# Other pads in on-chip memory before the activation tiles of a two-block model

## The chip, the cores and the metric

The kernel runs on one core of one Trainium2 chip. The metric is the device time of one execution in microseconds (us). Before the change the median of three runs is 1627.86 us (1627.2 to 1629.0). The activations are float32; the large matrix products are made with the fp32r form of TensorE, in which one product of two float32 operands is put together from three products of rounded parts.

## The reference, cut to what matters

Two blocks follow each other on 256 tokens of width 1024. The first has two layers; the second, one.

```
for l in range(2):
    x = x + 0.5 * swiglu(rms_norm(x), w_gate_up, w_down)      # 1024 -> 2*2816 -> 1024   (ffn1)
    u = rms_norm(x) @ w_in
    y = concat(ssd_mixer(u), mlstm_mixer(u), rwkv7_mixer(u))  # 2048 wide
    x = x + y @ w_out
    x = x + 0.5 * swiglu(rms_norm(x), w_gate_up, w_down)      # (ffn2)
x = rms_norm(x)
# second block, one layer, modulated by a vector c
h = rmsnorm(x) * (1 + sc1) + sh1
q, k, v, u, c_gate, b_gate = split(h @ w_in_2)
mixed = concat(rmsnorm(attention(q, k, v)), rmsnorm(b_gate * conv(c_gate * u)))
x = x + gt1 * (mixed @ w_out_2)
h = rmsnorm(x) * (1 + sc2) + sh2
val, gte = split(conv(h @ w_up_2))
x = x + gt2 * ((silu(gte) * val) @ w_down_2)
out = rmsnorm(x)
```

All weights are read once from HBM, as float32.

## The kernel before, in words

Activations lie transposed, features on the 128 partitions and the 256 tokens along the free dimension. The weights come in blocks of 128 x 128. Seven blocks form a chunk: `fetch` loads it into `raw` (SyncE's queue), `chunk` splits it with ScalarE into the rounded part `whi` (L134) and with VectorE into the rest `wlo` (L135). Four buffers of `whi` and four of `wlo` go round. `mm` makes three matmuls of one block and one activation tile (L153, L154, L155): high by high, high by low, low by high; each loads 128 columns of weights and streams 256 columns of activations. "Product" below means one such matmul. There are some 11,400 of them, and the program has 12,670 matmuls in all.

The activations of a product are split in the same way, and the high and the low part lie behind each other in one tile:

- `pair()` makes the input tiles of the dense products, under two names in turn. `pair1` holds the unnormalised input of the first four output tiles of a stage (`xg`: the products can start before the norm's statistics are there, and are scaled behind), `pair0` the normalised input (`xn`). For the second block's attention the normalised input lies in `pair1`.
- `hp` holds the hidden activations of a feed-forward stage (22 tiles of 128 features), the input of its down stage. Each of the five feed-forward stages has its own pool and its own `hp`.
- `m0`, `m1` hold the input of the second block's `w_out`; the first block's `w_out` inputs are tiles of the mixers' ring `w2` (`w` in the profile).
- `xgh`, `xgl` hold the second block's unnormalised inputs with two columns more (258).

Memory is given out from pools that are stacked: `const`, `weights`, `act`, then one pool for the stage (`ffn`, `mix`, `attn`), and from the second layer's ffn2 on a pool `later` below it, which holds the attention bias `ab` and `xgh`, `xgl`. `gap(pool, n)` takes n bytes of each partition from a pool and has GpSimd clear them (L261); nothing reads them. Its only effect is where the tiles behind it lie. The table `GAPS` sets n for each place.

The code's order sets the order of the work on each engine; there is no planner. Weights are taken from the front of the stream, so the down stage of a feed-forward follows its gate and up products without a break.

Of the kernel before, what the change touches and what calls it, by code (L numbers as in the profile page):

```python
# [37 lines left out]
GD_AHEAD = 1  # L38
BOOST = (1, 1, 1, 1, 1)
DENSE = 0.34  # L40
GAPS = {"xg": 448, "xn": 192, "mix": 288, "ffn": (384, 128, 448, 192, 448), "attn": 256}
W_OUT = ((("rwkv0", "rwkv1"), (12, 13, 14, 15)), (("ssd",), (0, 1, 2, 3, 4, 5, 6, 7)), (("mlstm",), (8, 9, 10, 11)))

IN_PAIRS = "k0 r0 v0 r2 k2 v2 xb8 xb0 dtg xb2 xb4 xb6 z0 z2 z4 xm0 z6 xm2 o0 o2".split()
# [33 lines left out]
def _program(tc, a, order, dbg=None):  # L78
# [5 lines left out]
    def pool(name, bufs=1, **kw):  # L84
        return es.enter_context(tc.tile_pool(name=name, bufs=bufs, **kw))
# [172 lines left out]
    def gap(pool, n):  # L258
        if n:
            turn.append(0)  # L260
            G.memset(pool.tile([128, n // 4], F32, name=f"gap{len(turn)}"), 0.0)  # L261
# [3 lines left out]
    def pair(dtype=F32R):  # L265
        pairs.append(0)
        return act.tile([128, 2, DT, T], dtype, name=f"pair{len(pairs) % 2}")
# [4 lines left out]
    def new_acc():  # L272
        return act.tile([128, 2, T], F32, name="acc", bufs=2)
# [47 lines left out]
    def ffn(l, which, acc, xg, next_gain):  # L321
        with tc.tile_pool(name=f"ffn{which}{l}", bufs=1) as fp:
            gu, dn = f"ffn{which}_w_gate_up", f"ffn{which}_w_down"
            gap(fp, GAPS["ffn"][2 * l + which - 1])
            hp = fp.tile([128, 2, FT, T], F32R, name="hp")
# [59 lines left out]
    def mixers(l, acc, xg):  # L385
# [10 lines left out]

        gap(mp, GAPS["mix"])
        nka = mp.tile([128, 4], F32, name="nka")
# [740 lines left out]
    def modulate(rb, gain, shift):  # L1139
        xn = pair()  # L1140
        for j in range(DT):
            n = tmp()[:, 0]
            V.scalar_tensor_tensor(n, x[:, j], gain[:, j:j + 1], rb, op0=OP.mult, op1=OP.mult)
            S.activation(xn[:, 0, j], n, AF.Identity, bias=shift[:, j:j + 1])
            V.scalar_tensor_tensor(xn[:, 1, j], n, shift[:, j:j + 1], xn[:, 0, j].bitcast(F32),
                                   op0=OP.add, op1=OP.subtract)
        return xn
# [12 lines left out]
    def second(accs, xg):  # L1160
        rb, rb2 = stat_rstd(accs, D, EPS, chain=True)
        with tc.tile_pool(name="attn", bufs=1) as mp:
            xn = modulate(rb2, a1[:, 0], mod[:, 0:8])
            gap(mp, GAPS["attn"])
            mixed = [mp.tile([128, 2, 4, T], F32R, name=f"m{i}") for i in range(2)]
# [102 lines left out]
        with tc.tile_pool(name="ffn_2", bufs=1) as fp:  # L1268
            rb, = stat_rstd([acc], D, EPS)
            xn = modulate(rb, a1[:, 1], mod[:, 24:32])  # L1270
            gap(fp, GAPS["ffn"][4])
            hp = fp.tile([128, 2, FT, T], F32R, name="hp")
# [40 lines left out]
    acc = new_acc()  # L1313
    gap(act, GAPS["xg"])
    xg = pair()
    gap(act, GAPS["xn"])
    for j in range(0, DT, 2):
# [8 lines left out]
    later = None  # L1326
    for l in range(LAYERS):
        acc, xg = ffn(l, 1, acc, xg, f"mix_norm{l}")
        dbg(f"xa{l}", x)
        acc, xg = mixers(l, acc, xg)  # L1330
        dbg(f"xb{l}", x)
        if l == LAYERS - 1:
            later = pool("later")
            ab = later.tile([128, 8, 384], F32, name="ab")
        acc, xg = ffn(l, 2, acc, xg, f"ffn1_norm{l + 1}" if l + 1 < LAYERS else None)
        dbg(f"xc{l}", x)
# [161 lines left out]
```

## Time and profile before

| | |
|---|---|
| median of three runs | 1627.86 us |
| profiled execution | 1627.1 us, span 1625.3 us |
| TensorE busy with matmuls | 1584.9 us, 13,660 instructions |
| VectorE, ScalarE, GpSimd busy | 1161.4, 1000.1, 47.5 us |
| mean granted TensorE clock | 0.989 of full speed |
| HBM read | 287.51 MB, 178 GB/s over the span |

The profiled execution takes 1.8 us more than the span from its first to its last instruction. The share of busy time of TensorE counts pipelined matmuls, so it tells that a matmul was under way, not how densely they follow each other. How densely is read from the starts: in a stretch where products follow each other without a wait, the time from the first to the last start over the number of products in between is the pace, in ns for one product. In a row of the view by tile, the starts are those of every third product (the lines L153, L154 and L155 take turns), so n instructions of one line span 3(n - 1) steps.

### The profile page before, as it was taken

The numbers are of one execution on the slowest core, as the hardware profiler recorded it, in microseconds if no ns is written. First come the engines' busy times: TensorE is split into PE (matmuls) and PEld (weight loads), VectorE is DVE, ScalarE is ACT, GpSimd is POOL, SyncE is SP. The second block draws the span as 40 slices with busy tenths as digits, with TensorE's granted clock in tenths as the row PEclk, the third lists the DMA queues.
The fourth block names the chain that finished last, engine by engine and source line by source line (L and its number), as shares of the span: only waits on it lengthen the run. The fifth ranks groups of instructions, "written<-read, shape, count | busy, mean of one in ns | idle before, by whom it ended". The sixth has DMA issues, their size and how long they took to land.

```text
span 1625.3 us, 33775 instructions
## 1 busy us (share of the span) xinstructions
PE 1584.9 (98%) x13660; PEld 1516.4 (93%) x13660; DVE 1161.4 (71%) x1965; ACT 1000.1 (62%) x1692; POOL 47.5 (3%) x68
## 2 busy tenths in 40 slices
PE   8999999999999999999999899999999999999998
PEld 7999988878999999999998887799999998999997
DVE  7865679856787755787568975688785676798853
ACT  6554576887655454545458788765554566587753
POOL 0000001000000000000000100000000000000000
PEclk9999989999999999999999999999999999999999
DMA  7866633333357766597563333436886653556662
GB/s 252 306 195 190 204 118 123 101 112 116 115 181 244 242 187 194 185 329 260 183 194 125 115 106 117 127 117 216 288 306 185 185 166 113 159 162 190 187 189 72
DMA packets 106717, 290.81 MB, mean 179 GB/s; under 512 B 15640, under 2 KB 28096, under 8 KB 106432
## 3 DMA queue, kind: packets, MB, share of 16 engines
q1 hardware_dynamic: 106272, 288.12, 55.9%
q8 instruction: 107, 1.75, 0.4%
q10 hardware_dynamic: 288, 0.52, 0.1%
q14 instruction: 50, 0.41, 0.1%
HBM read 287.51 MB, written 1.09 MB: 178 GB/s over the span
## 4 chain that ended last, share of the span: by engine, by line
PE 77%; issue 13%; DVE 5%; ACT 2%; DMA 1%; POOL 1%; SPq 0%; DVEq 0%; POOLq 0%; ACTq 0%
PE d L155 21%; PE d L153 21%; PE d L154 21%; DVE wlo L135 1%; DMA ada<-ada 1%; PE m L691 1%; PE m L754 1%; PE m L1064 1%; POOL stm L212 1%; PE m L1068 1%; PE m L736 1%; PE st L221 1%; PE m L705 1%; ACT whi L134 1%; PE m L1066 1%
## 5 line engine op out<-in xcount | busy, mean ns | idle before, releaser
L135 DVE TENSOR_TENSOR wlo<-raw,whi 128x896 fp32r<-128x896 f32 x544 | 590.4, 1089 | 245.1 <-ACT whi L134 242.3
L153 PE MATMUL d<-pair,whi 128*128 128x256 f32 x2672 | 753.2, 282 | 4.8 <-ACT whi L134 2.1
L155 PE MATMUL d<-pair,wlo 128*128 128x256 f32 x2672 | 753.8, 282 | 1.8 <-DVE wlo L135 1.8
L154 PE MATMUL d<-pair,whi 128*128 128x256 f32 x2672 | 752.9, 282 | 0.1
L134 ACT CAST whi<-raw 128x896 fp32r<-128x896 f32 x544 | 511.5, 943 | 348.3 <-PE d L154 254.0
L153 PEld LDWEIGHTS d<-pair,whi 128*128 128x128 f32 x2672 | 508.8, 190 | 14.8 <-issue 5.9
L155 PEld LDWEIGHTS d<-pair,wlo 128*128 128x128 f32 x2672 | 508.1, 190 | 7.2 <-DVE wlo L135 2.9
L154 PEld LDWEIGHTS d<-pair,whi 128*128 128x128 f32 x2672 | 508.5, 190 | 3.0 <-issue 1.4
L154 PE MATMUL d<-hp,whi 128*128 128x256 f32 x880 | 246.6, 280 | 0.0
L155 PE MATMUL d<-hp,wlo 128*128 128x256 f32 x880 | 246.1, 280 | 0.0
L153 PE MATMUL d<-hp,whi 128*128 128x256 f32 x880 | 246.1, 280 | 0.0
L155 PEld LDWEIGHTS d<-hp,wlo 128*128 128x128 f32 x880 | 166.2, 189 | 0.0
L154 PEld LDWEIGHTS d<-hp,whi 128*128 128x128 f32 x880 | 166.1, 189 | 0.0
L153 PEld LDWEIGHTS d<-hp,whi 128*128 128x128 f32 x880 | 166.1, 189 | 0.0
L205 ACT CAST hp<-h 128x256 fp32r<-128x256 f32 x88 | 35.4, 406 | 90.9 <-DVE h L345 90.8
L1124 DVE SCALAR_TENSOR_TENSOR adasum<-ada,sc,adasum 128x1024 f32<-128x1024 f32 x42 | 53.8, 1281 | 14.4 <-DMA ada<-ada 14.4
L206 DVE TENSOR_TENSOR hp<-h,hp 128x256 fp32r<-128x256 f32 x88 | 36.7, 421 | 15.3 <-ACT hp L205 14.5
L1157 DVE SCALAR_TENSOR_TENSOR up<-raw,par,up 128x255 f32<-128x255 f32 (+1 forms) x88 | 37.2, 480 | 10.6 <-ACT raw L1153 10.3
L344 ACT ACTIVATE s<-d 128x256 f32<-128x256 f32 x80 | 30.2, 378 | 23.3 <-PE d L155 22.2
L345 DVE TENSOR_TENSOR h<-s,d 128x256 f32<-128x256 f32 x88 | 36.0, 415 | 3.8 <-ACT s L344 3.8
L155 PE MATMUL d<-w,wlo 128*128 128x256 f32 x128 | 37.1, 290 | 0.0
L154 PE MATMUL d<-w,whi 128*128 128x256 f32 x128 | 37.1, 290 | 0.0
(403 smaller groups left out, 1829.0 us busy)
## 6 DMA issues: line engine op xcount, KB each, us to landing
raw<-ws SPq DMA_DIRECT2D x544, 448.0 KB, 3.7
ada<-ada SPq DMA_DIRECT2D x48, 512.0 KB, 5.9
w<-da SPq DMA_DIRECT2D x16, 256.0 KB, 5.1
w<-small SPq DMA_DIRECT2D x10, 256.0 KB, 3.9
ab<-abias SPq DMA_DIRECT2D x1, 1536.0 KB, 7.1
x<-xT SPq DMA_DIRECT2D x4, 256.0 KB, 4.9
w<-da SPq DMA_DIRECT2D x8, 128.0 KB, 3.6
w<-dw SPq DMA_DIRECT2D x4, 256.0 KB, 5.5
```

The source lines that it names most:

```text
L134: S.copy(hi, raw)
L135: V.tensor_sub(lo, raw, hi.bitcast(F32))
L153: PE.matmul(p, h, xh, start=start, stop=False, skip_group_check=True)
L154: PE.matmul(p, h, xl, start=False, stop=False, skip_group_check=True)
L155: PE.matmul(p, lo, xh, start=False, stop=stop, skip_group_check=True)
L205: S.copy(hi, src)
L206: V.tensor_sub(lo, src, hi.bitcast(F32))
L212: G.tensor_tensor(dst, m, mhalf.to_broadcast([128, n]), op=OP.pow)
L344: S.activation(s, p[:, 0], AF.Silu)
L345: V.tensor_mul(h, s, p[:, 1])
L1124: V.scalar_tensor_tensor(acc, w, sc[:, k:k + 1], acc, op0=OP.mult, op1=OP.add)
L1157: V.scalar_tensor_tensor(dst[:, i, d:], raw[:, i, :T - d], P(w, 3 * j + k), dst[:, i, d:], op0=OP.mult, op1=OP.add)
```

## The change

The pads are set anew, and the pool `later` gets one. Nothing else is changed.

```diff
-GAPS = {"xg": 448, "xn": 192, "mix": 288, "ffn": (384, 128, 448, 192, 448), "attn": 256}
+GAPS = {"xg": 192, "xn": 192, "mix": 32, "ffn": (128, 128, 128, 0, 0), "attn": 0, "later": 256}
...
         if l == LAYERS - 1:
             later = pool("later")
+            gap(later, GAPS["later"])
             ab = later.tile([128, 8, 384], F32, name="ab")
```

The five numbers of `"ffn"` belong to layer 0's ffn1 and ffn2, layer 1's ffn1 and ffn2, and the second block's feed-forward. From them follow the start addresses, in bytes in each partition, as the built programs place the tiles. All eight weight buffers stay where they are; each of their blocks is 512 bytes long and begins at remainder 160 when divided by 256. The steps inside the activation tiles (1024 bytes from one feature tile to the next) keep the remainder of the first.

| tile (products) | before, remainder by 256 (by 512) | after, remainder by 256 (by 512) |
|---|---|---|
| `pair1` (1,056) | 93536: 96 (352) | 93280: 96 (96) |
| `pair0` (6,960) | 112224: 96 (96) | 111968: 96 (352) |
| `hp`, layer 0, ffn1 (528) | 129120: 96 (96) | 128608: 96 (96) |
| `hp`, layer 0, ffn2 (528) | 128864: 96 (352) | 128608: 96 (96) |
| `hp`, layer 1, ffn1 (528) | 129184: **160** (160) | 128608: **96** (96) |
| `hp`, layer 1, ffn2 (528) | 157728: **32** (32) | 157536: **96** (352) |
| `hp`, second block (528) | 157984: **32** (288) | 157536: **96** (352) |
| `w2`, eight in each layer (384) | 96 (96) | 96 (96) |
| `m0`, `m1` (192) | 157792, 165984: 96 (96) | 157536, 165728: 96 (352) |
| `xgh`, `xgl` (192) | 141024, 149280 | the same |

On TensorE, VectorE, ScalarE and SyncE the instructions stand in the same order as before. On GpSimd there are eight clearings of pads where there were ten. The next piece is GpSimd's order from the end of layer 1's mixers to the end of the program, before (-) and after (+), with the semaphores that an instruction waits for; `gap` is a pad, `stm` the statistics of a norm.

```order
-L261 MEMSET gap_13771 128x48 [waits DMAHW3_49,DMAHW1_49,DMAHW5_49,DMAHW0_49,DMAHW6_49,DVE_49,DMAHW7_49,PE_49,Pool_49]
-L212 TENSOR_TENSOR stm<-stm,mhalf 128x2 [waits DVE_49]
-L261 MEMSET gap_16201 128x64 [waits DMAHW2_49,DMAHW3_49,DMAHW1_49,DMAHW4_49,DMAHW0_49,DMAHW5_49,DVE_49,DMAHW7_49,PE_49,Pool_49]
+L261 MEMSET gap_13767 128x64 [waits DMAHW3_49,DMAHW1_49,DMAHW5_49,DMAHW0_49,DMAHW6_49,DVE_49,DMAHW7_49,PE_49,Pool_49]
+L212 TENSOR_TENSOR stm<-stm,mhalf 128x2 [waits DVE_49] x3
+L212 TENSOR_TENSOR stm<-stm,mhalf 128x2 [waits DVE_49,Pool_49] x2
 L212 TENSOR_TENSOR stm<-stm,mhalf 128x2 [waits DVE_49] x2
-L212 TENSOR_TENSOR stm<-stm,mhalf 128x2 [waits DVE_49,Pool_49] x2
-L261 MEMSET gap_17620 128x112 [waits DVE_49,PE_49]
-L212 TENSOR_TENSOR stm<-stm,mhalf 128x2 [waits DVE_49] x2
```

Of the three pads that stood here one is left, that of the pool `later`; the seven root calculations on the statistics are all still there, in the same order.

## Rows read from the trace of the kernel before

**Rows 1.** The page: span, TensorE's busy time, the chain that ended last.

```profile
span 1625.3 us, 33775 instructions
...
PE 1584.9 (98%) x13660; PEld 1516.4 (93%) x13660; DVE 1161.4 (71%) x1965; ACT 1000.1 (62%) x1692; POOL 47.5 (3%) x68
...
PE 77%; issue 13%; DVE 5%; ACT 2%; DMA 1%; POOL 1%; SPq 0%; DVEq 0%; POOLq 0%; ACTq 0%
```

**Rows 2.** Busy time by stretch; three down stages, then the last gate and up stage.

```profile
core 0: us, PE busy (x) PEld busy (x) DVE busy (x) ACT busy (x) POOL busy (x), PEclk, DMA share, GB/s
...
136.40:196.00 59.60, 59.60 (x528) 59.60 (x527) 34.83 (x42) 29.13 (x39) 0.00 (x0) 1.00 0.63 194
783.10:845.40 62.30, 62.30 (x521) 62.30 (x520) 34.55 (x42) 28.42 (x37) 0.00 (x0) 1.00 0.59 183
1243.20:1305.50 62.30, 62.30 (x528) 62.30 (x527) 36.76 (x47) 31.44 (x45) 0.00 (x0) 1.00 0.61 184
1455.00:1550.80 95.80, 95.80 (x815) 95.80 (x815) 83.47 (x152) 73.75 (x131) 0.00 (x0) 1.00 0.60 185
```

**Rows 3.** Tile hp, TensorE: count, ns min/median/max, first and last start (us).

```profile
L153 PE MATMUL d<-hp,whi x176: 276/276/276, 136.3 to 195.8; 128*128 128x256 f32 x176
...
L153 PE MATMUL d<-hp,whi x176: 276/276/276, 598.6 to 658.1; 128*128 128x256 f32 x176
...
L153 PE MATMUL d<-hp,whi x176: 280/283/283, 782.3 to 845.3; 128*128 128x256 f32 x176
...
L153 PE MATMUL d<-hp,whi x176: 279/281/285, 1243.1 to 1305.4; 128*128 128x256 f32 x176
...
L153 PE MATMUL d<-hp,whi x47: 279/281/285, 1551.0 to 1567.4; 128*128 128x256 f32 x47
...
L154 PE MATMUL d<-hp,whi x48: 279/281/362, 1569.1 to 1585.9; 128*128 128x256 f32 x48
```

**Rows 4.** Tiles pair, w and m, TensorE, uninterrupted stretches; the columns of rows 3.

```profile
L154 PE MATMUL d<-pair,whi x274: 276/276/282, 31.0 to 123.8; 128*128 128x256 f32 x137
...
L154 PE MATMUL d<-pair,whi x31: 276/276/282, 480.4 to 490.6; 128*128 128x256 f32 x31
...
L154 PE MATMUL d<-pair,whi x15: 276/276/369, 1238.0 to 1242.8; 128*128 128x256 f32 x15
...
L154 PE MATMUL d<-pair,whi x31: 281/281/281, 1125.4 to 1136.0; 128*128 128x256 f32 x31
...
L153 PE MATMUL d<-pair,whi x32: 281/281/281, 1320.6 to 1331.5; 128*128 128x256 f32 x32
...
L153 PE MATMUL d<-pair,whi x272: 281/281/384, 1454.8 to 1550.6; 128*128 128x256 f32 x136
...
L153 PE MATMUL d<-w,whi x32: 281/281/281, 462.6 to 473.5; 128*128 128x256 f32 x32
```

**Rows 5.** Groups by line, 136.3 to 196.3 us: count, busy us, mean ns, idle before.

```profile
L135 DVE TENSOR_TENSOR wlo<-raw,whi 128x896 fp32r<-128x896 f32 x26 | 28.4, 1092 | 23.2 <-ACT whi L134 23.1
L134 ACT CAST whi<-raw 128x896 fp32r<-128x896 f32 x26 | 24.6, 945 | 29.8 <-PE d L154 25.7 <-issue 3.5 <-ACT pair L302 0.3
```

**Rows 6.** Line L345, layer 0's and layer 1's ffn1; the columns of rows 3.

```profile
L345 DVE TENSOR_TENSOR h<-s,d x21: 411/414/422, 31.1 to 133.0; 128x256 f32<-128x256 f32 x21
...
L345 DVE TENSOR_TENSOR h<-s,d x21: 409/414/422, 675.0 to 777.9; 128x256 f32<-128x256 f32 x21
```

**Rows 7.** Groups by line on GpSimd, whole span; the columns of rows 5.

```profile
L212 POOL TENSOR_TENSOR stm<-stm,mhalf 128x2 f32<-128x2 f32 (+1 forms) x14 | 13.4, 957 | 356.5 <-DVE stm L238 347.2 <-DVE xgl L206 4.9 <-DVE stm L230 3.7
...
L261 POOL MEMSET gap<- 128x112 f32 (+5 forms) x10 | 1.5, 162 | 803.2 <-PE d L155 782.6 <-PE m L155 20.3 <-POOLq L1489 0.3
```

## The prediction

> **What bounds the kernel.** I read the page's head and chain first, then the busy time by stretch, then single tiles on TensorE. The page says that TensorE is busy 98% of the span and that 77% of the chain that ended last is its matmuls [rows 1]. Such a share doesn't tell how densely the matmuls follow each other. In the three down stages of rows 2 TensorE is busy without a hole (59.60 of 59.60 us, 62.30 of 62.30 us twice) at a granted clock of 1.00, its higher level of 2.4 GHz, while VectorE and ScalarE are busy 35 to 37 and 28 to 31 us, and the DMA engines 0.59 to 0.63 [rows 2]. So nothing is waited for there, and the time of such a stage is its number of products times their pace. Yet the same 528 products of the same shape take different times.
>
> The pace of each down stage comes from rows 3: 176 instructions of one line are 175 steps of three products, 525 products.
>
> - layer 0, ffn1 (`hp` at remainder 96): (195.8 - 136.3) / 525 = 113.3 ns
> - layer 0, ffn2 (remainder 96): (658.1 - 598.6) / 525 = 113.3 ns
> - layer 1, ffn1 (remainder 160, that of the weights): (845.3 - 782.3) / 525 = 120.0 ns
> - layer 1, ffn2 (remainder 32): (1305.4 - 1243.1) / 525 = 118.7 ns
> - second block (remainder 32): (1567.4 - 1551.0) / 138 = 118.8 ns, and behind the next break (1585.9 - 1569.1) / 141 = 119.1 ns
>
> Remainders here are by 256. By 512 the two fast tiles lie at 96 and at 352 and have one pace, so 256 is the period that the rows support.
>
> Placement isn't all of it. Tiles that lie at 96 throughout have two paces [rows 4]: `pair` at 31.0 to 123.8 makes 92.8 / 819 = 113.3 ns, at 1454.8 to 1550.6 95.8 / 813 = 117.8 ns, and the mixers' `w` at 462.6 (10.9 / 93) 117 ns with 0.1 us of rounding. The median duration of one shows which it is, 276 or 281 ns. The pace is taken at a stretch's beginning and mostly kept until a wait breaks it. Of the eight stretches of `pair` with over 400 products in a row, the first and last of which are the first and sixth row of rows 4, seven have the fast pace. In short ones it is less even: the products behind the norm's statistics at ffn2's start (`pair1`, then `pair0`) run fast in layer 0 (480.4 to 490.6, 10.2 / 90) and slow at the corresponding place of layer 1 (1125.4 to 1136.0, 10.6 / 90) [rows 4]. I call them fast (113.3) and slow (117.8).
>
> **The change, part by part.** By 256, three tiles move in relation to the weights: the `hp` of layer 1's ffn1 (160 to 96), of its ffn2 and of the second block (32 to 96). All other inputs of products keep their remainder by 256; several move by 256.
>
> 1. Layer 1's ffn1 down. Its products follow without a break from `pair`, which has the fast pace in all long stretches of both layers but the second block's, and at 96 both down stages that follow fast products keep it [rows 3]. 63.0 us become 59.5: -3.5 us. At the slow pace it would be 528 x (120.0 - 117.8) = -1.2 us.
> 2. Layer 1's ffn2 down. The products before it run at 276 ns, the fast pace (1238.0 to 1242.8) [rows 4]. 62.3 us become 59.5: -2.8 us; at the slow pace -0.5 us.
> 3. The second block's down. The products before it run slow [rows 4], so the first 142, up to the first break by transposes, take the slow pace: 142 x 0.9 ns = -0.1 us. The other 386 begin anew behind each of four breaks. All fast would be 386 x 5.4 = -2.1 us, all slow -0.3 us. Seven long stretches in eight speak for one end, the pair at 480.4 and 1125.4 for a coin; I take two thirds fast, -1.5 us. Together -1.6 us.
> 4. The tiles that move by 256 or more with the remainder kept: 0. `pair1` at 352 by 512 runs at both paces (slow at 1320.6), `pair0` at 96 by 512 too (slow at 1454.8, fast at 31.0) [rows 4], so neither place excludes one. The bounds are in the rivals.
> 5. VectorE and ScalarE tiles in the feed-forward pools move in relation to 256 as well. L345 takes 414 ns in the median in layer 0's and in layer 1's ffn1, whose pools stood 64 apart [rows 6]: 0. The second block's pool alone has the conv of the up stage; a change of its speed would meet a VectorE that is busy 83.5 of 95.8 us beside a full TensorE [rows 2], so it stays covered up to some 12 us.
> 6. Two clearings fewer on GpSimd: all ten take 1.5 us [rows 7], each at a stage's turn, on an engine that then idles until VectorE has the statistics ready; its 14 root calculations waited 347 of 356 us for VectorE [rows 7]. Value 0, at most 0.3 us (two of 162 ns) either way. The new clearing in `later` stands where one of the removed stood, with the same engines in its wait; only the root calculations are queued behind it.
>
> What becomes late next: a faster down stage wants a chunk every 21 x 113.3 = 2.38 us. Splitting one takes 945 ns on ScalarE and 1092 ns on VectorE, on two engines and with four buffers, and layer 0's ffn1 down did so for 26 chunks [rows 5] with TensorE never idle [rows 2]. So the cover holds.
>
> Sum: 3.5 + 2.8 + 1.6 = 7.9 us off the profiled execution's own 1627.1 us: 1619.2 us. The median of the runs stands 0.8 us above the profiled one, which makes 1620.0 us.
>
> A rule of the Trainium skill speaks against this. Rows 3 show that one and the same product takes 113.3, 118.7 or 120.0 ns. TensorE: Matmul & The Clock Gate (Step-by-step: what each phase is for) says that TensorE has two independent read ports, one for the streamed operand and one for the weights, and that loading the next weights takes no read bandwidth from the running matmul; SBUF — State Buffer (Who interferes with whom) adds that TensorE never waits on anyone. By that rule no placement could matter and the sum would be 0. The trace disagrees as to the paces, which differ by 6.7 ns in stages where nothing else is waited for.
>
> **The rivals.**
>
> - *The pace belongs to the stage, and the change does nothing* (5%). Then the three slow down stages would be slow for what comes with them. For it: all three lie in the program's second half. Against it: the `pair` products right before layer 1's ffn2 down run at 276 ns and the `hp` products right behind at 281 [rows 3, 4], with the same weights' buffers and engines. Time 1627.9 us.
> - *The moved tiles get the slow pace, or other stretches fall into it* (11%). The time of every later stretch shifts, so its pace is drawn anew; the difference between 480.4 and 1125.4 shows that this happens. All moved tiles slow: 1.2 + 0.5 + 0.5 = 2.2 us, 1625.7 us. One long stretch that falls from fast to slow costs 4.5 ns x 430 = 1.9 us; two of them beside the full gain give 1623.8 us.
> - *The second block's up products become fast* (12%). 960 x 4.5 ns = 4.3 us more, and the first part of its down stage with them 0.6 us: 1615.1 us. For it: seven of eight. Against it: they come behind the 258 wide products of `xgh` and `xgl`, which stay where they are, and slow in the same way at 1320.6 behind such products [rows 4].
> - *Slower: the period is 512 and not 256* (5%). Then `pair0`, moved from 96 to 352 by 512, loses the fast pace at its entries. The price is 4.5 ns for each of its 6,960 products that now run fast; from 7.9 us / 4.5 ns = 1,760 on the change loses, and with 5,000 of them it would end at 1620.0 + 22.5 = 1642.5 us. For it: `pair1`, at 352 before, is slow at 1125.4 and 1320.6 [rows 4]. Against it: the same tile at 352 is fast at 480.4 [rows 4], and `hp` of layer 0's ffn2, also at 352, makes 113.3 ns over all 528 [rows 3].
>
> **How the numbers follow.** The forecast has 67%, with a range of its own of 1617.5 to 1622.0 us: 1.1 us down if all of step 3's later products and one of the smaller slow stretches turn fast, 1.2 us up if they turn slow, and about 1 us for draws elsewhere and for the runs' spread (1627.2 to 1629.0). Less than 0.2%, some 3.3 us, can't be told from no change here; that bound is 1624.6 us. Faster by more: the forecast, the fast up stage and a little of the second rival, 81%. Within: most of the second rival and the first, 13%. Slower: the last and a bad draw, 6%. The range of 8 in 10 goes from the fast up stage at 1615.1 to the forecast with two long stretches lost, 1623.8 us.
>
> **What would show it.** Right: the first starts to the last of `hp` in layer 1's two down stages span 59.5 us, median 276 ns. Step 3 shows in the medians behind each break, 276 or 281. Step 4 is wrong if `pair` stretches that ran at 276 run at 281 in numbers, above all layer 0's, before which nothing changes in time; step 5, if L345's median leaves 414 ns; step 6, if a root calculation starts late behind a clearing. The whole is wrong if `hp` at 96 in layer 1 still takes 118 to 120 ns.

## The result and the profile after

The changed kernel takes 1617.47 us (median of four runs, 1614.81 to 1619.38) against 1628.02 us (1627.2 to 1629.0): a ratio of 0.9934, 95% interval 0.9917 to 0.9951. The forecast was 1620.0 us with a range of 1615.1 to 1623.8; its own narrower range began at 1617.5, just above what was measured. The profiled execution takes 1618.35 us, 8.75 us less than that of before.

The page of the changed kernel (busy time and instructions by engine; the span is 1616.6 us):

```profile
PE 1575.4 (97%) x13660; PEld 1507.1 (93%) x13660; DVE 1161.2 (72%) x1965; ACT 999.5 (62%) x1692; POOL 47.0 (3%) x66
```

As in [rows 1], TensorE is busy nearly all the time, with the same 13,660 matmul instructions. What changed is how densely they follow each other. Tile `hp` on TensorE, changed kernel, the down stages in the order of [rows 3] (columns as there):

```profile
L153 PE MATMUL d<-hp,whi x176: 276/276/276, 138.0 to 197.5; 128*128 128x256 f32 x176
...
L153 PE MATMUL d<-hp,whi x176: 276/276/276, 595.6 to 655.1; 128*128 128x256 f32 x176
...
L153 PE MATMUL d<-hp,whi x176: 276/276/276, 779.3 to 838.8; 128*128 128x256 f32 x176
...
L153 PE MATMUL d<-hp,whi x176: 276/276/276, 1241.2 to 1300.7; 128*128 128x256 f32 x176
...
L153 PE MATMUL d<-hp,whi x48: 276/276/276, 1544.7 to 1560.6; 128*128 128x256 f32 x48
...
L154 PE MATMUL d<-hp,whi x48: 276/276/367, 1562.0 to 1578.1; 128*128 128x256 f32 x48
```

The first two stages are as before. The two of layer 1 now span 59.5 us as well, where they spanned 63.0 and 62.3, and the second block's makes 15.9 / 141 = 112.8 ns, with 0.1 us of rounding. All have a median of 276 ns. The stretches of `pair` tell of the rest (line L155, then L153 three times):

```profile
L155 PE MATMUL d<-pair,wlo x136: 276/276/281, 29.7 to 75.6; 128*128 128x256 f32 x136
...
L153 PE MATMUL d<-pair,whi x137: 278/281/281, 77.6 to 125.7; 128*128 128x256 f32 x137
...
L153 PE MATMUL d<-pair,whi x32: 281/281/281, 1315.9 to 1326.8; 128*128 128x256 f32 x32
...
L153 PE MATMUL d<-pair,whi x271: 276/276/279, 1452.5 to 1544.3; 128*128 128x256 f32 x136
```

Layer 0's first up stage, fast throughout before (the first row of [rows 4]), is slow here in its second half. The break between its halves is a wait: a product waited 0.9 us for VectorE's split of its weights (L135).

The second block's up stage has gone the other way: slow in the sixth row of [rows 4], fast here. And the mixers drew another clock. Busy time by stretch, before:

```profile
225.00:262.00 37.00, 33.99 (x241) 30.18 (x240) 29.32 (x60) 24.26 (x44) 5.38 (x7) 0.82 0.38 119
870.00:907.00 37.00, 34.34 (x282) 31.66 (x281) 32.53 (x63) 28.28 (x50) 5.57 (x7) 0.95 0.39 125
```

and after:

```profile
225.00:262.00 37.00, 34.36 (x281) 31.33 (x281) 33.61 (x68) 28.20 (x52) 5.89 (x7) 0.95 0.45 139
870.00:907.00 37.00, 35.53 (x253) 31.93 (x253) 29.42 (x61) 25.02 (x45) 5.89 (x7) 0.82 0.36 115
```

The granted clock (the column before the last two) was 0.82 in layer 0's stretch and 0.95 in layer 1's, and the other way round after; at 0.95 TensorE has 29 to 40 matmuls more in the same 37 us.

Where the 8.75 us went is read from TensorE's starts of the same products in both traces. At the start of layer 1's ffn1 down the changed kernel was 3.0 us ahead, behind it 6.5 (-3.5); its ffn2 down took the lead from 1.9 to 4.7 (-2.8); the second block's up, behind its first 144 products, from 2.7 to 6.3 (-3.6), its down to 8.7 (-2.4). The rest nearly cancels: +1.7 us up to the end of layer 0's ffn1 up, -4.6 from there to the end of layer 0's ffn2, nearly all of it in the mixers, +4.6 in layer 1's mixers, and +2.0 around 1400 us, where the granted clock of the stretch from 1400 to 1405 us was 0.66, against 1.00 before.

### The profile page after: what moved, and what is told of

Its sections match the earlier page's. It is cut to its first block, busy times and chain, and to the rows that moved or that the text cites. A ratio compares the mean times of both kernels' runs of the same rounds, so it can differ in the third digit from the quotient of the medians.

```text
span 1616.6 us, 33765 instructions
## 1 busy us (share of the span) xinstructions
PE 1575.4 (97%) x13660; PEld 1507.1 (93%) x13660; DVE 1161.2 (72%) x1965; ACT 999.5 (62%) x1692; POOL 47.0 (3%) x66
## 4 chain that ended last, share of the span: by engine, by line
PE 79%; issue 13%; DVE 5%; ACT 2%; POOL 1%; DMA 0%; DVEq 0%; POOLq 0%; SPq 0%; ACTq 0%
PE d L155 22%; PE d L153 21%; PE d L154 21%; DVE wlo L135 1%; PE m L691 1%; PE m L754 1%; PE m L1064 1%; POOL stm L212 1%; PE m L1068 1%; PE m L736 1%; PE st L221 1%; PE m L705 1%; ACT whi L134 1%; PE m L1066 1%; PE m L601 1%
## 5 line engine op out<-in xcount | busy, mean ns | idle before, releaser
L135 DVE TENSOR_TENSOR wlo<-raw,whi 128x896 fp32r<-128x896 f32 x544 | 590.2, 1089 | 237.1 <-ACT whi L134 233.1
L153 PE MATMUL d<-pair,whi 128*128 128x256 f32 x2672 | 751.8, 282 | 5.2 <-ACT whi L134 2.4
L155 PE MATMUL d<-pair,wlo 128*128 128x256 f32 x2672 | 752.4, 282 | 3.0 <-DVE wlo L135 3.0
L153 PEld LDWEIGHTS d<-pair,whi 128*128 128x128 f32 x2672 | 506.8, 190 | 14.9 <-issue 5.9
L155 PEld LDWEIGHTS d<-pair,wlo 128*128 128x128 f32 x2672 | 507.3, 190 | 8.3 <-DVE wlo L135 4.0
L154 PE MATMUL d<-hp,whi 128*128 128x256 f32 x880 | 243.5, 277 | 0.0
L155 PE MATMUL d<-hp,wlo 128*128 128x256 f32 x880 | 242.9, 276 | 0.0
L153 PE MATMUL d<-hp,whi 128*128 128x256 f32 x880 | 242.9, 276 | 0.0
L155 PEld LDWEIGHTS d<-hp,wlo 128*128 128x128 f32 x880 | 165.2, 188 | 0.0
L153 PEld LDWEIGHTS d<-hp,whi 128*128 128x128 f32 x880 | 165.2, 188 | 0.0
L345 DVE TENSOR_TENSOR h<-s,d 128x256 f32<-128x256 f32 x88 | 36.1, 415 | 4.0 <-ACT s L344 4.0
L155 PE MATMUL d<-w,wlo 128*128 128x256 f32 x128 | 37.2, 291 | 0.0
```

The lines of the kernel that those rows point to most:

```text
L135: V.tensor_sub(lo, raw, hi.bitcast(F32))
L153: PE.matmul(p, h, xh, start=start, stop=False, skip_group_check=True)
L154: PE.matmul(p, h, xl, start=False, stop=False, skip_group_check=True)
L155: PE.matmul(p, lo, xh, start=False, stop=stop, skip_group_check=True)
L345: V.tensor_mul(h, s, p[:, 1])
```

## The experiments

The theory: the pace of a product follows from the distance, by 256 bytes, between its streamed tile and its weights; where the distance allows two paces, an entry behind a wait draws one. The rivals: the pace belongs to the stage; moves by 256 count too; the tile's own place counts and not the distance.

**Five places in one kernel.**

```diff
-"ffn": (128, 128, 128, 0, 0)
+"ffn": (160, 96, 32, 96, 128)
```

> The changed kernel, but with the hidden tile hp of the five feed-forward stages at five other remainders by 256: 128, 64, 0, 192 and 224 in program order (weights stay at 160). My theory, that the pace of a product depends on the distance between its streamed tile and its weights by 256: each down stage has its own pace, constant over its 528 products, and layer 0's two, which made 113.3 ns at 96, leave it or at least take other slow values than 117.8 ns; 528 products span 59.5 us (113.3 ns) to 63 us (120 ns). Rival, that the pace belongs to the stage: layer 0's down stages stay at 113.3 ns, and the last three go back to 118 to 120 ns or stay at 113.3, whatever the remainder.

Tile `hp`, the five down stages, at remainders 128, 64, 0, 192 and 224:

```profile
L153 PE MATMUL d<-hp,whi x176: 277/281/285, 136.0 to 198.1; 128*128 128x256 f32 x176
...
L153 PE MATMUL d<-hp,whi x176: 277/280/282, 597.0 to 658.6; 128*128 128x256 f32 x176
...
L153 PE MATMUL d<-hp,whi x176: 278/281/285, 784.9 to 847.9; 128*128 128x256 f32 x176
...
L153 PE MATMUL d<-hp,whi x176: 277/279/281, 1245.8 to 1307.0; 128*128 128x256 f32 x176
...
L153 PE MATMUL d<-hp,whi x48: 279/279/279, 1552.5 to 1569.1; 128*128 128x256 f32 x48
```

118.3, 117.3, 120.0, 116.6 and 117.7 ns. Layer 0's stages lost their 113.3 ns, so the pace doesn't belong to the stage. With [rows 3], all eight multiples of 32 have been seen with weights at 160, and 96 is the only one with 113.3 ns. The one execution took 1628.16 us.

**Everything shifted by 64, the weights too.**

```diff
     acc = new_acc()
+    gap(const, 64)
     gap(act, GAPS["xg"])
```

> The changed kernel with everything behind the constants moved up by 64 bytes, the weights with it: weights at remainder 224, activations at 160, their distance as in the changed kernel. If the distance decides, the five down stages keep 113.3 ns (59.5 us from the first to the last of 526 products). If the activation tile's own remainder decides, they take 120 ns (63 us), which is what a tile at 160 had in the kernel before.

Tile `hp` at 160, weights at 224, layer 1's ffn1 down:

```profile
L153 PE MATMUL d<-hp,whi x176: 276/276/276, 779.7 to 839.2; 128*128 128x256 f32 x176
```

59.5 us at the very remainder that took 63.0 before. All four stages of the first block did the same, and the first two parts of the second block's; behind later breaks that one had the slow pace, 117.8 ns. The one execution took 1615.54 us. At this shift the distance decides, not the place; only this shift was run.

**Only the three tiles, and all but them.**

```diff
 # the kernel before, with
-"ffn": (384, 128, 448, 192, 448)
+"ffn": (384, 128, 384, 256, 256)
 # the changed kernel, with
-"ffn": (128, 128, 128, 0, 0)
+"ffn": (128, 128, 192, 192, 192)
```

> The kernel before with nothing moved but the three hp tiles (layer 1's ffn1 and ffn2, the second block), to remainder 96; all other pads as before. My theory: the whole gain is here, so 1617 to 1620 us, within 2 us of the changed kernel, and the three down stages at 113.3 ns (the last one perhaps in part at 117.8). Rival, that moves by 256 of pair0 and pair1 carry a part of it (of the 10.5 us gained, 7.9 were forecast from the three tiles): 1620 to 1623 us.

> The changed kernel with the three hp tiles put back to remainders 160, 32 and 32, all other pads as changed. My theory: the time of the kernel before, 1628 us within 2 us, with the down stages at 120.0, 118.7 and 118.7 ns. Rival (moves by 256 count): 1623 to 1626 us.

With only the three tiles moved: 1614.65 us, ratio to before 0.9943 (0.9928 to 0.9958). With all but them: 1626.42 us, ratio 1.0015 (1.0003 to 1.0028). The kernel before ran beside both at 1624.66 us and not at 1628, so the first expectation's 1617 to 1620 us is missed by 2.4 us, but the ratio fits, and the second lies in its range: the three tiles carry the whole gain, within the width of the intervals, and the moves by 256 gain nothing. Tile `hp` of layer 1's ffn1 with only the three moved:

```profile
L153 PE MATMUL d<-hp,whi x176: 276/276/277, 778.0 to 837.5; 128*128 128x256 f32 x176
```

and with all but the three, there and for layer 1's ffn2:

```profile
L153 PE MATMUL d<-hp,whi x176: 280/283/284, 779.2 to 842.2; 128*128 128x256 f32 x176
...
L153 PE MATMUL d<-hp,whi x176: 279/281/286, 1242.0 to 1304.3; 128*128 128x256 f32 x176
```

The old paces of [rows 3] are back at their places, 120.0 and 118.7 ns.

**A finer sweep.** `hp` gets 64 elements more, and its halves begin some bytes in:

```diff
-hp = fp.tile([128, 2, FT, T], F32R, name="hp")
+t = fp.tile([128, 2 * n + 64], F32R, name="hp")      # n = FT * T
+h, q = HP_HI[s] // 4, n + HP_LO[s] // 4              # bytes, per stage s
+hp = [t[:, o:o + n].rearrange("p (k t) -> p k t", k=FT) for o in (h, q)]
```

> The changed kernel, but with hp of the five feed-forward stages at remainders 112, 104, 80, 88 and 100 in program order (16 or fewer bytes from 96). If the paces of the coarse sweep are points of a smooth curve with its best at 96, neighbours by 4 or 8 bytes stay near 113.3 ns and those by 16 lie between 113.3 and 117 to 118; if 96 is hit only by chance and a better place lies between, one of the five runs below 113.3 ns. If the chip reads in lines and only the line counts, neighbours within a line are equal to 113.3 ns.

Tile `hp`, layer 0's two down stages, at 112 and at 104 (the line is L155 in this file):

```profile
L155 PE MATMUL d<-hp,whi x176: 278/282/288, 138.9 to 201.4; 128*128 128x256 f32 x176
...
L155 PE MATMUL d<-hp,whi x176: 282/282/283, 605.1 to 668.1; 128*128 128x256 f32 x176
```

119.0 and 120.0 ns; 80, 88 and 100 made 119.2, 120.0 and 121.3 ns. All three guesses fell: there is no smooth curve around 96, nothing better at these five places beside it, and four bytes are already too much. None of the five is a multiple of 32, and no run moved the weights by so little; whether the distance or the start itself costs the time here stays open.

**The low half alone.** The same code, with the high half left at 96.

> The changed kernel with the low half of hp (read by one product in three, that of the high weights with the low activations) at remainders 128, 64, 32, 160 and 224 in program order, the high half at 96 throughout. If each product's pace goes by its own tile's distance, only one in three gets slower: a third of the coarse sweep's loss, 113.3 + (118.3 - 113.3) / 3 = 115.0, 114.7, 115.1, 115.5 and 114.8 ns. If the three products of a block are locked to each other, the pace goes to 116 ns or more with one of them misplaced. A pace under 113.3 ns would point to a better layout than the changed one.

Tile `hp`, layer 0's ffn1 down, low half at 128:

```profile
L155 PE MATMUL d<-hp,whi x176: 276/281/285, 137.4 to 199.8; 128*128 128x256 f32 x176
```

118.9, 117.7, 118.9, 119.2 and 117.7 ns at 128, 64, 32, 160 and 224. One misplaced product in three costs about what three do. The two products of a block that still read the high half at 96 are slowed with it: from their start to the next one's they took 115.5 to 121.1 ns in the mean of a stage. So the paces of the three aren't independent, as the second guess had it. No stage came under 113.3 ns.

**The changed kernel again.**

> The changed kernel once more, unchanged. My theory: the slow pace of 117.8 ns at remainder 96 is drawn anew at each entry and kept until a wait, so the time varies by a few us between executions and the stretches of over 400 products that are slow are others than in the first profile (there, the second half of layer 0's ffn1 up); ratio to before 0.9925 to 0.9955. Rival, that the entry fixes it: the same stretches are slow as in the first profile, and the times agree within 1 us.

Ratio 0.9943 (0.9923 to 0.9963), runs from 1616.05 to 1624.25 us. Tile `pair` in layer 0's ffn1 up and layer 1's ffn2 up:

```profile
L155 PE MATMUL d<-pair,wlo x274: 276/276/277, 31.0 to 123.8; 128*128 128x256 f32 x137
...
L154 PE MATMUL d<-pair,whi x145: 278/281/281, 1133.3 to 1184.2; 128*128 128x256 f32 x145
```

The stretch that was slow in the first profile is fast, and the two long ones of layer 1's ffn2 up, fast there, are slow: the one shown and the next (1186.7 to 1236.6). The same program draws anew at these entries, and its times spread over 8 us.

Not every entry draws. The 138 products of `pair` and the 96 of `w` behind them at the end of the mixers were slow in both layers in all ten traces of this case; in [rows 4] `w` at 462.6 is one of them. Here (tile `w`, layer 0):

```profile
L153 PE MATMUL d<-w,whi x32: 281/281/281, 462.6 to 473.6; 128*128 128x256 f32 x32
```

For such entries the rival stands, and no run varied what fixes them. And no long down stage drew the slow pace: all 24 with `hp` at 96, or at the same distance, ran at 113.3 ns, and of the 16 with all or half of `hp` elsewhere none was under 116.6. So a slow draw doesn't explain the slow places of the sweeps.

**The 258 wide tiles at 96.**

```diff
-"later": 256
+"later": 128
...
-xg = [later.tile([128, DT, T + 2], F32R, name=f"xg{n}") for n in "hl"]
+xg = [later.tile([128, DT, 320], F32R, name=f"xg{n}")[:, :, :T + 2] for n in "hl"]
...
-g2 = fp.tile([128, T], F32, name="g2", bufs=2)
+g2 = fp.tile([128, T], F32, name="g2", bufs=1 if (l, which) == (LAYERS - 1, 2) else 2)
```

> The changed kernel with xgh and xgl of the second block at remainder 96 too: their feature tiles are 1280 bytes apart instead of 1032, of which 258 columns are used as before (the temporary g2 of the last feed-forward has one buffer for it, to make room). Their 192 products ran at about 120 to 121 ns and came before slow stretches. If the distance rule holds for them, they run at 114 ns (258 columns), 192 x 6.5 ns = 1.2 us less, and up to 1.2 us more if the stretches behind them become fast: ratio 0.998 to 0.9995 against the changed kernel. Rival, that a stream of 258 columns has the slow pace wherever it lies: no change of the pace.

The rival was right on their pace. The mean of 172 steps between starts of such products is 120.9 ns, against 119.9 in the changed kernel. But the two stretches behind them, 96 products at the attention's start and 144 at the up stage's, slow in all nine other traces, ran fast (tile `pair`, line L153):

```profile
L153 PE MATMUL d<-pair,whi x32: 276/276/288, 1312.6 to 1323.2; 128*128 128x256 f32 x32
...
L153 PE MATMUL d<-pair,whi x48: 276/276/282, 1430.6 to 1446.6; 128*128 128x256 f32 x48
```

That is 240 x 4.5 ns = 1.1 us, the second part of the expectation, seen in one trace; so the place of the wide products seems to set the pace of what follows them, though not their own. The times can't show so little: 1620.38 us (1611.25 to 1626.73), ratio 0.9954 (0.9930 to 0.9978), beside 0.9943 and 1618.99 us for the changed kernel; the expected ratio of 0.998 to 0.9995 between the two was not seen. No version better than the changed one was shown.

## Why the prediction was right, and where its sizes were off

1. and 2. Layer 1's two down stages: -3.5 and -2.8 us forecast, 63.0 and 62.3 us became 59.5 in the rows of `hp`. Right in mechanism and size.
3. The second block's down: -1.6 us forecast, -2.4 measured. The term rested on a slow first part and one third of the later ones slow; in this execution all five parts are fast. In the five traces with `hp` there at 96 or at its distance the first part was always fast and 12 of the 20 later ones, and the stage was 1.2 to 2.4 us shorter than before. So the step's size is a draw, as the text said, and 1.6 lies among its values.
4. The moves by 256: 0 forecast. The ratio of 1.0015 for all but the three says no gain, and at most 0.28% of loss. `pair0` at 352 by 512 ran fast in the second block's up (1452.5 to 1544.3). The period-512 rival is out. The sign named for a failure of this step did appear, in layer 0's ffn1 up (281 ns from 77.6 us on), but the same program ran fast there the next time, so it was a draw and not the place.
5. and 6. L345's median stays at 414 ns (22 instances from 672.0 us on), and GpSimd's eight clearings take 0.9 us instead of 1.5. TensorE waited 5.9 us for root calculations in both traces, so nothing got late behind them.

The step that failed is the forecast's slow up stage in the second block, against which the rival had 12%. I took its pace as fixed by the 258 wide products before it, and with it that of the first part of the down stage. Behind the wide products only the first 144 were slow, up to a wait (and fast where the wide tiles were moved); the 815 behind that were fast in all nine profiles taken later. Among them are both halves of the change by themselves: only the three tiles moved (1447.4 to 1539.7, 276 ns), and the old `hp` places (all but the three moved, tile `pair`):

```profile
L154 PE MATMUL d<-pair,whi x272: 276/276/282, 1457.0 to 1549.2; 128*128 128x256 f32 x136
```

So neither half needs the other for a fast up stage, and the likely reading is that the profile of before had caught an unlucky draw there: -3.6 us of the profiled difference that are not the change's. That kernel was profiled only once, so this isn't shown. The other draws of paces and of the clock happen to cancel it within 0.1 us, so it is luck that the profiled 8.75 us are the three tiles' 8.7. On the runs' medians, draws of this kind and the clock's in the mixers make the time uncertain by some us: the kernel before ran from 1620.57 to 1635.2 us in the last comparison. Whether the 10.5 us of the first comparison hold more than the 8.7 us of the three tiles (3.5 + 2.8 + 2.4) can't be told from four runs each; the last comparison, with 12 and 23 runs, gives 9.5 us.

The Trainium skill's rule that was weighed, independent read ports for the streamed operand and the weights (TensorE: Matmul & The Clock Gate, Step-by-step: what each phase is for), would have made all these paces one. The runs show 113.3 to 121.3 ns for one product, by where `hp` lies. Why, they don't show: that the two reads get into each other's way is the likely reading, and it was only argued.

## What to carry to other kernels

Where TensorE is busy without a hole, read the pace from the starts of its matmuls, tile by tile: two stages with the same work and other times are a hint on placement. The distance of the streamed tile from the weights is set by a pad of some hundred bytes and was worth 5.6% of a stage (63.0 to 59.5 us); a sweep with another pad in each stage measures many places in one run, but the value found holds for this shape, its type and its order of products. One profile of such a kernel is in part one draw of the paces; before a stage's state is taken as fixed, profile the same kernel twice.

## What the runs showed of the hardware

- With weights at 160 by 256, products of 128 x 256 float32 in the fp32r form took 113.3 ns a step (or 117.8, by the entry) at 96, and 113.3 at 160 with the weights at 224; 120.0 at 160 and at 0; 118.7 at 32, 117.3 at 64, 118.3 at 128, 116.6 at 192, 117.7 at 224; and 119.0 to 121.3 at 80, 88, 100, 104 and 112.
- The two paces at 96 are kept over hundreds of products; the change from one to the other was seen only at waits. Some entries had either pace from trace to trace; those at the end of the mixers were slow in all ten. The matmul's duration (276 or 281 ns) shows the pace without counting.
- 258 columns took 119.7 to 120.9 ns at the places tried, some 7 ns more than 256 at the best one.
- The granted clock in the mixers differed between two profiles by place (0.82 and 0.95 in the stretches shown), although TensorE's instructions stand in the same order.
